# RWKV-7 chunks with both heads of a pair in one instruction, and inverse roots on GpSimd

## The chip, the cores and the metric

The kernel runs as one program on one core of a Trainium2 chip. The metric is the device time of one execution in microseconds (us); several runs were timed and the median is used. Beside the timed runs there is one execution taken with the hardware profiler. All times of single instructions come from it.

## The reference, cut to what matters

Two layers are computed on an input of 1024 positions by 1024 channels in float32. Layer 0 (RG-LRU and HGRN2) is not touched by the change. Layer 1 is RWKV-7 time mixing: 16 heads of 64 channels, each with a 64 x 64 state that is updated position by position:

```python
def step(state, inp):
    r_t, w_t, k_t, v_t, al_t, be_t = inp
    sa = jnp.einsum("bhvk,bhk->bhv", state, al_t)
    state = (state * w_t[:, :, None, :] + sa[..., None] * be_t[:, :, None, :]
             + v_t[..., None] * k_t[:, :, None, :])
    return state, jnp.einsum("bhvk,bhk->bhv", state, r_t)
...
y = ((y - mean) * lax.rsqrt(var + RW_GN_EPS)).reshape(bsz, seq, RW_WIDTH) * ln_w + ln_b
bonus = jnp.sum(r * k * r_k, axis=-1, keepdims=True) * v
y = y + bonus.reshape(bsz, seq, RW_WIDTH)
return (y * jax.nn.silu(g)) @ w_out
...
x = x + rms_norm(mix, post_norm[layer])
```

The mean and the variance of y are those of one head at one position.

## The kernel before, in words

The recurrence is not run position by position. The 1024 positions are cut into 16 chunks of 64, and within a chunk the recurrence is solved with matrix products and one inverted triangular 64 x 64 matrix per head. The heads are worked on in eight pairs; in a pair, head 0 lies on partitions 0 to 63 and head 1 on partitions 64 to 127. In the code `e` is the pair (0 to 7), `h` the head in the pair, `ch` the chunk.

Earlier stages (up to about 1380 us) have written to DRAM: `ard`, for each chunk the scaled vectors A (64 columns) and R (64 columns) of each head; `bkd`, the scaled vectors B and K, where head 0 has B in columns 0 to 63 and K in 64 to 127, and head 1 the other way round; `vd`, the values; and `abf`, from which `invert` and `merge` make the inverses `ytd` in the background. `egc` holds, for each chunk, the decay of each channel over the whole chunk.

The last stage is `chain_phase` (L1024). For each chunk it runs:

- `values` (L1399): loads the values into `SV` and the inverse into `YTc`. `SV` has for each head a stack of 128 partitions: the 64 rows of the state on the head's own half, the 64 values on the other half.
- `gram` (L1412), one chunk ahead: loads `GM` (A and R) and `BK`, and multiplies for each head BK against [A R] (L1428; 64 rows of contraction, 128 weight columns, 128 streamed columns, one PSUM bank per head and group of four pairs). VectorE masks the results with `gm`: the K part goes back into the other half of `GM` (L1433), the part that belongs to B and R into `RB` (L1434). These are four instructions for each group of four pairs, eight for a chunk. GpSimd scales BK by the chunk's decay into `BS` (L1438), and TensorE transposes `BS` (L1443); ScalarE copies it to `NK` (L1444).
- `chain` (L1447), the sequential part: since state and values are stacked, one product with 128 rows of contraction and 64 weight columns gives the right sides (L1456), and another of the same shape starts the outputs (L1461). ScalarE copies the right sides to `B` (L1458). GpSimd scales the old state into `se` (L1467, one instruction for each head). The inverse is applied (L1471), its result takes the values' place of the solved part in `SV` (L1473: head 0 by VectorE, head 1 by ScalarE). A product with `NK` (L1478) gives what the chunk adds to the state, and VectorE adds `se` and writes the next chunk's `SV` (L1480, one instruction for each head). The last product (L1483) completes the outputs, ScalarE copies them (L1486), and they go to DRAM.
- `norm` (L1492) normalizes the outputs of a chunk, `turn` (L1524) transposes them, and `project` (L1536) multiplies two chunks at a time by the output weights and adds the normalized result to x. Both use `rstd2` (L197) for 1/sqrt: a scaling on VectorE, a root on ScalarE (L202), a reciprocal and one Newton step on VectorE (L201, L203 to L206). There is also `rstd` (L189), used in layer 0: two GpSimd instructions (L193, L194), the second a power with exponent -0.5.

Each matrix product of float32 operands shows as two records in the profile, so the 16 products of a step (8 pairs, 2 heads) are 32 records; a transpose is one.

The order: `chain` and `gram` are generators, and `chain_phase` advances them in five steps per chunk. Between these it calls `background` (inverses and merges) and takes one piece of `fill`. The fill is the gate's projection (`gpiece`, L1014, products at L184 to L186) until chunk 8, and the output projection (`project`, L1550 to L1552) from chunk 9. The framework then orders each engine's instructions by a simulated timeline and these priorities, with raised priority for the chain of chunks 14 and 15. Each engine runs its list in order. PSUM has eight banks, shared out by `BANKS` (L1392); the load queue is SyncE's (SP).

Of the kernel before, what the change touches and what calls it, by code (L numbers as in the profile page):

```python
# [7 lines left out]
F32 = mybir.dt.float32  # L8
# [3 lines left out]
ALU = mybir.AluOpType  # L12
# [33 lines left out]
class Net:  # L46
# [977 lines left out]
    def chain_phase(self, cx, mp, vg, n):  # L1024


        nc, a = self.nc, self.a
# [20 lines left out]
        self.SV, self.YTc, self.G, self.Y, self.yd = {}, {}, {}, {}, [self.dram.tile([P, HALF], F32, name=f"yd{i}") for i in range(16)]  # L1048
# [8 lines left out]
        nc.gpsimd.memset(self.SV[0][0:64, 0], 0.0)  # L1057
        nc.gpsimd.memset(self.SV[0][64:128, 1], 0.0)
# [308 lines left out]
    def chain_consts(self):  # L1367
        nc, big = self.nc, self.big

        gm = big.tile([P, P], F32, name="gm")  # L1370
        for lo_, base in ((0, 0), (64, 64)):
            m = big.tile([P, P], F32, name="mask_g", tag="BS")
            mv = m.rearrange("p (a b) -> p a b", b=64)
            nc.gpsimd.memset(m, 1.0)
            nc.gpsimd.affine_select(out=mv, in_=mv, pattern=[[1, 2], [1, 64]], compare_op=ALU.is_ge, fill=0.0,
                                    base=base - 1, channel_multiplier=-1)
            nc.vector.tensor_copy(gm[lo_:lo_ + 64, :], m[lo_:lo_ + 64, :])
        self.gm = gm
# [13 lines left out]
    BANKS = {"pg": ("g", 2), "pt": ("t", 1), "pq": ("t", 1), "pi": ("t", 1), "pc": ("c", 2), "py": ("y", 1),  # L1392
# [18 lines left out]

    def gram(self, ch):  # L1412
        nc = self.nc
        GM = self.cc[ch % 2].tile([P, 2, KT, P], F32, name="GM")
        for h in range(2):
            hs = slice(64 * h, 64 * h + 64)
            nc.sync.dma_start(out=GM[hs, h], in_=self.ard[ch, hs])
        BK = self.big.tile([P, KT, P], F32, name="BK")
        nc.sync.dma_start(out=BK, in_=self.bkd[ch])
        RB = self.cc[ch % 2].tile([P, KT, 64], F32, name="RB")  # L1420
        bc = lambda x, n: x.rearrange("p (o t) -> p o t", o=1).broadcast_to([n, 4, x.shape[-1]])
        yield
        for eg in range(2):
            ps = [self.bank("pg").rearrange("p (q t) -> p q t", t=P) for _ in range(2)]
            for q in range(4):
                for h in range(2):
                    hs = slice(64 * h, 64 * h + 64)
                    nc.tensor.matmul(ps[h][:, q, :], lhsT=BK[hs, eg * 4 + q, :], rhs=GM[hs, h, eg * 4 + q, :],  # L1428
                                     start=True, stop=True)
            for h in range(2):  # L1430
                es = slice(eg * 4, eg * 4 + 4)
                b, k = slice(64 * h, 64 * h + 64), slice(64 - 64 * h, 128 - 64 * h)
                nc.vector.tensor_mul(GM[k, h, es, :], ps[h][k], bc(self.gm[k, :], 64))  # L1433
                nc.vector.tensor_mul(RB[b, es, :], ps[h][b, :, 64:128], bc(self.gm[b, 64:128], 64))  # L1434
            yield
        BS = self.big.tile([P, KT, P], F32, name="BS", tag="BS")
        eg_ = self.egc[:, ch, :].rearrange("p (e o) -> p e o", o=1).broadcast_to([P, KT, P])
        nc.gpsimd.tensor_mul(BS, BK, eg_)  # L1438
        NK = self.cc[ch % 2].tile([P, KT, P], F32, name="NK")
        for eg in range(2):  # L1440
            ps = self.bank("pt").rearrange("p (q t) -> p q t", t=P)
            for q in range(4):
                nc.tensor.transpose(ps[:, q, :], BS[:, eg * 4 + q, :], self.ident)  # L1443
            nc.scalar.copy(NK[:, eg * 4:eg * 4 + 4, :], ps)  # L1444
        self.G[ch] = GM, RB, NK

    def chain(self, ch):  # L1447
        nc = self.nc
        GM, RB, NK = self.G.pop(ch)
        SV, YT = self.SV.pop(ch), self.YTc.pop(ch)  # L1450
# [3 lines left out]
        ps = pv(self.bank("pc"))  # L1454
        for e, h in eh:
            nc.tensor.matmul(ps[H[h], e, :], lhsT=GM[:, h, e, 0:64], rhs=SV[:, h, e, :], start=True, stop=True)  # L1456
        B = self.cc[ch % 2].tile([P, KT, 64], F32, name="B")
        nc.scalar.copy(B, ps)  # L1458
        py = pv(self.bank("py"))
        for e, h in eh:  # L1460
            nc.tensor.matmul(py[H[h], e, :], lhsT=GM[:, h, e, 64:128], rhs=SV[:, h, e, :], start=(e == 0), stop=False,  # L1461
                             skip_group_check=True)
        if ch < 15:
            se = self.cc[ch % 2].tile([P, KT, 64], F32, name="se")
            for h in range(2):
                eg = self.egc[H[h], ch, :].rearrange("p (e o) -> p e o", o=1).broadcast_to([64, KT, 64])
                nc.gpsimd.tensor_mul(se[H[h]], SV[H[h], h], eg)  # L1467
        yield
        ps = pv(self.bank("pc"))
        for e, h in eh:  # L1470
            nc.tensor.matmul(ps[H[h], e, :], lhsT=YT[H[h], e, :], rhs=B[H[h], e, :], start=True, stop=True)  # L1471
        for h in range(2):
            (nc.scalar.copy if h else nc.vector.tensor_copy)(SV[H[h], h], ps[H[h]])  # L1473
        yield
        if ch < 15:
            ps = pv(self.bank("pc"))
            for e, h in eh:
                nc.tensor.matmul(ps[H[h], e, :], lhsT=NK[:, e, H[h]], rhs=SV[:, h, e, :], start=True, stop=True)  # L1478
            for h in range(2):
                nc.vector.tensor_add(self.SV[ch + 1][H[h], h], ps[H[h]], se[H[h]])  # L1480
        yield
        for e, h in eh:
            nc.tensor.matmul(py[H[h], e, :], lhsT=RB[H[h], e, :], rhs=SV[H[h], h, e, :], start=False, stop=(e == KT - 1),  # L1483
                             skip_group_check=True)
        y = self.cc[ch % 2].tile([P, HALF], F32, name="B")
        nc.scalar.copy(y, py.rearrange("p e v -> p (e v)"))  # L1486
# [5 lines left out]
    def norm(self, ch):  # L1492

        nc, gp = self.nc, self.gp
# [24 lines left out]
        r = self.rstd2(gp, va, KT, 1.0 / 64, GN_EPS)  # L1519
# [16 lines left out]
    def project(self, tt):  # L1536
# [28 lines left out]
        r = self.rstd2(gp, s1, 1, 1.0 / D, EPS)  # L1565
# [57 lines left out]
```

## Time and profile before

| | |
|---|---|
| median of 3 runs | 1886.89 us (1884.31 to 1889.57) |
| profiled execution, own time | 1885.01 us |
| its span, first to last instruction | 1882.9 us |
| TensorE matmul (PE) busy | 1737.0 us, 92% |
| TensorE weight load (PEld) busy | 1462.9 us, 78% |
| VectorE (DVE) busy | 1212.2 us, 64% |
| ScalarE (ACT) busy | 795.6 us, 42% |
| GpSimd (POOL) busy | 695.8 us, 37% |

How to read it: a row of the groups view names a line of the kernel, the engine, the operation, `out<-in`, the shapes and the count, and then the busy time in us, the mean of one instruction in ns, and the engine's idle time before them with what ended it. A TensorE shape such as `64*128 64x128` means 64 rows of contraction by 128 weight columns, and 64 rows by 128 streamed columns. Matmul records overlap, since the unit is pipelined: the time that a group takes is read from its start to the start of what follows, not from the records' lengths. PEclk is the share of its full clock that TensorE was granted.

### The profile page before, as it was taken

How to read it: one execution, taken by the hardware profiler on the slowest of the kernel's cores; microseconds unless marked ns; L12 is line 12 of the kernel's file. 1: busy time of each engine (PE TensorE's matmuls, PEld its weight loads, DVE VectorE, ACT ScalarE, POOL GpSimd, SP SyncE). 2: the span in 40 equal slices, each digit the busy share in tenths (PEclk: the TensorE clock that was granted, in tenths of full speed). 3: DMA queues.
4: the chain of work that ended last, by engine and by line, in shares of the span. 5: the costliest groups of instructions: out<-in, count | busy, mean ns of one | idle time of the engine just before them, and what ended most of it. 6: DMA issues, size and time to landing. Idle time of an engine off the chain costs nothing. (4 is left out here: it accounts for less than half of the span.)

```text
span 1882.9 us, 36336 instructions
## 1 busy us (share of the span) xinstructions
PE 1737.0 (92%) x14418; PEld 1462.9 (78%) x14418; DVE 1212.2 (64%) x2213; ACT 795.6 (42%) x1550; POOL 695.8 (37%) x618
## 2 busy tenths in 40 slices
PE   8989989999899999999999999978679999997888
PEld 6879789787897777777878766668678998875776
DVE  6485483675847889745354686786593434359985
ACT  5322222323226655445454765764453433432221
POOL 5534232333222212465434244554441425425430
PEclk9999999999899999999999999979878998988989
DMA  5101101111022111365235276654565655544531
GB/s 181 45 23 46 56 19 63 46 35 41 18 73 85 53 60 67 125 238 169 101 123 185 89 171 167 173 130 113 121 164 139 170 148 165 156 132 150 181 106 62
DMA packets 218313, 206.56 MB, mean 110 GB/s; under 512 B 133280, under 2 KB 162208, under 8 KB 218144
## 3 DMA queue, kind: packets, MB, share of 16 engines
q1 hardware_dynamic: 216992, 200.04, 35.5%
q0 software_dynamic: 1152, 4.19, 0.7%
q8 instruction: 114, 1.87, 0.4%
q14 instruction: 55, 0.45, 0.1%
HBM read 136.22 MB, written 67.96 MB: 108 GB/s over the span
## 5 line engine op out<-in xcount | busy, mean ns | idle before, releaser
L135 POOL TENSOR_TENSOR wl<-w,wh 128x1024 fp32r<-128x1024 f32 x110 | 276.5, 2520 | 291.6 <-ACT wh L133 283.2
L160 PE MATMUL mm<-xh,wh 128*128 128x512 f32 x768 | 306.3, 400 | 0.2
L162 PE MATMUL mm<-xh,wl 128*128 128x512 f32 x768 | 305.3, 398 | 0.0
L161 PE MATMUL mm<-xl,wh 128*128 128x512 f32 x768 | 304.1, 396 | 0.0
L184 PE MATMUL mm<-wh,xh 128*128 128x256 f32 x560 | 169.8, 304 | 7.5 <-ACT xh L149 3.7
L160 PEld LDWEIGHTS mm<-xh,wh 128*128 128x128 f32 x768 | 146.0, 190 | 35.3 <-issue 3.6
L162 PEld LDWEIGHTS mm<-xh,wl 128*128 128x128 f32 x768 | 145.9, 190 | 34.5 <-issue 4.1
L161 PEld LDWEIGHTS mm<-xl,wh 128*128 128x128 f32 x768 | 145.9, 190 | 33.2 <-issue 3.4
L186 PE MATMUL mm<-wh,xl 128*128 128x256 f32 x560 | 166.4, 300 | 4.9 <-DVE xl L150 4.9
L133 ACT CAST wh<-w 128x1024 fp32r<-128x1024 f32 x112 | 117.7, 1051 | 124.2 <-PE mm L161 54.8
L185 PE MATMUL mm<-wl,xh 128*128 128x256 f32 x560 | 165.7, 296 | 0.0
L184 PEld LDWEIGHTS mm<-wh,xh 128*128 128x128 f32 x560 | 114.5, 205 | 10.7 <-ACT xh L149 4.3
L186 PEld LDWEIGHTS mm<-wh,xl 128*128 128x128 f32 x560 | 113.6, 204 | 7.0 <-DVE xl L150 6.3
L185 PEld LDWEIGHTS mm<-wl,xh 128*128 128x128 f32 x560 | 114.2, 204 | 0.9
L803 DVE SCALAR_TENSOR_TENSOR mix<-ut,vec,mix 128x512 f32<-128x512 f32 x64 | 62.5, 985 | 39.9 <-ACT mix L802 39.1
L1438 POOL TENSOR_TENSOR BS<-BK,egc 128x1024 f32<-128x1024 f32 x16 | 31.7, 1980 | 139.5 <-PE pt L1443 70.7
L184 PE MATMUL po<-wh,xh 128*128 128x256 f32 x256 | 75.7, 296 | 1.6 <-DVE vg L1021 1.6
L420 DVE COPY_PREDICATED ST<-m_l,sm 64x128 f32<-64x128 uint8 x224 | 72.5, 337 | 5.5
L185 PE MATMUL po<-wl,xh 128*128 128x256 f32 x256 | 75.2, 294 | 0.0
L186 PE MATMUL po<-wh,xl 128*128 128x256 f32 x256 | 74.8, 292 | 0.0
L1428 PE MATMUL pg<-GM,BK 64*128 64x128 f32 x512 | 58.0, 308 | 9.4 <-DMA BK<-bkd 4.8
L1295 DVE TENSOR_TENSOR PR<-YP,BL 128x64 f32<-128x64 f32 (+14 forms) x60 | 57.5, 973 | 11.2 <-POOL BL L1285 10.4
(378 smaller groups left out, 4332.6 us busy)
## 6 DMA issues: line engine op xcount, KB each, us to landing
w<-in_W SPq DMA_DIRECT2D x112, 512.0 KB, 3.8
ard<-AR SPq DMA_DIRECT2D x16, 512.0 KB, 4.1
BK<-bkd SPq DMA_DIRECT2D x16, 512.0 KB, 3.7
vd<-vg SPq DMA_DIRECT2D x32, 256.0 KB, 2.7
GM<-ard SPq DMA_DIRECT2D x32, 256.0 KB, 4.4
x<-in_x SPq DMA_DIRECT2D x8, 512.0 KB, 9.8
mgd<-sgq SPq DMA_DIRECT2D x16, 256.0 KB, 2.1
ut<-mgd SPq DMA_DIRECT2D x16, 256.0 KB, 4.1
```

What stands on the lines that cost most here:

```text
L133: nc.scalar.copy(hi, w)
L135: (nc.vector if first else nc.gpsimd).tensor_sub(lo, w, hi.bitcast(F32))
L160: nc.tensor.matmul(ps, lhsT=wh[:, c:c + P], rhs=a, start=(k == 0), stop=False)
L161: nc.tensor.matmul(ps, lhsT=wh[:, c:c + P], rhs=b, start=False, stop=False)
L162: nc.tensor.matmul(ps, lhsT=wl[:, c:c + P], rhs=a, start=False, stop=(k == KT - 1))
L184: nc.tensor.matmul(ps, lhsT=a, rhs=h, start=(k == 0), stop=False)
L185: nc.tensor.matmul(ps, lhsT=a, rhs=l, start=False, stop=False)
L186: nc.tensor.matmul(ps, lhsT=b, rhs=h, start=False, stop=(k == KT - 1))
L420: nc.vector.copy_predicated(d, m, x)
L803: nc.vector.scalar_tensor_tensor(out, sh, self.v(f"mu{p}", k), out, ALU.mult, ALU.add)
L1295: nc.vector.tensor_mul(fv(PR, 0, [[16 * n, 2], [n, 16], [1, n]]), fv(YP, 0, [[256, 2], [16, 16], [1, n]]), fv(BL, i, [[256, 2], [0, 16], [ ...
L1428: nc.tensor.matmul(ps[h][:, q, :], lhsT=BK[hs, eg * 4 + q, :], rhs=GM[hs, h, eg * 4 + q, :], start=True, stop=True)
```

## The change

The masks now cover both heads, so that a PSUM bank that holds both is masked by one instruction. `gram` multiplies in two steps: K against [A R] (64 weight columns, 128 streamed), both heads into one bank, masked by one instruction per group of four pairs into `KG`; and B against R (64 by 64) for all eight pairs into one bank, masked by one instruction into `RB`. For head 1 the halves of [A R] are swapped when loaded, with two loads. The scaling of BK is gone: BK itself is transposed, and not for the last chunk. State and values are no longer stacked: `V` has the values, `UV` the values and the solved part, and one tile `S` the state of both heads. In `chain`, each head has a PSUM bank `pa[h]`. A product with `KG` (64 rows of contraction, 128 weight columns, 64 streamed) starts right sides and outputs at once, and one with `AR` and `S` adds the state's share (not in chunk 0). Copies of right sides and outputs are one instruction per head on ScalarE, as both copies of the solved part are now. The state is updated by one add and one multiplication for both heads on VectorE. `norm` and `project` call `rstd` in the place of `rstd2`. The banks: "pc" has one buffer in the place of two, "py" two in the place of one.

```diff
 chain_phase:
-        nc.gpsimd.memset(self.SV[0][0:64, 0], 0.0)
-        nc.gpsimd.memset(self.SV[0][64:128, 1], 0.0)
 chain_consts:
-        for lo_, base in ((0, 0), (64, 64)):
-            m = big.tile([P, P], F32, name="mask_g", tag="BS")
+        rm = big.tile([P, 64], F32, name="rm")
+        for lo_, base, step in ((0, -1, 1), (64, 64, -1)):
+            m = big.tile([P, P], F32, name="mask_g")
...
+            nc.vector.tensor_copy(rm[lo_:lo_ + 64, :], m[lo_:lo_ + 64, 64 - lo_:128 - lo_])
+        self.gm, self.rm = gm, rm
+        self.S = big.tile([P, KT, 64], F32, name="S")
-    BANKS = {"pg": ("g", 2), "pt": ("t", 1), "pq": ("t", 1), "pi": ("t", 1), "pc": ("c", 2), "py": ("y", 1),
+    BANKS = {"pg": ("g", 2), "pt": ("t", 1), "pq": ("t", 1), "pi": ("t", 1), "pc": ("c", 1), "py": ("y", 2),
 values:
-            o = 64 - 64 * h
-            nc.sync.dma_start(out=SV[o:o + 64, h].rearrange("p e v -> p (e v)"),
-                              in_=self.vd[ch * 64:(ch + 1) * 64, 0, h * HALF:(h + 1) * HALF])
+            src = self.vd[ch * 64:(ch + 1) * 64, 0, h * HALF:(h + 1) * HALF]
+            for v, o in ((V, 64 * h), (UV[:, h], 64 - 64 * h)):
+                nc.sync.dma_start(out=v[o:o + 64].rearrange("p e v -> p (e v)"), in_=src)
 gram:
-            nc.sync.dma_start(out=GM[hs, h], in_=self.ard[ch, hs])
+        nc.sync.dma_start(out=AR[H[0]], in_=self.ard[ch, H[0]])
+        for x in range(2):
+            nc.sync.dma_start(out=AR[H[1], :, H[1 - x]], in_=self.ard[ch, H[1], :, H[x]])
...
-                    nc.tensor.matmul(ps[h][:, q, :], lhsT=BK[hs, eg * 4 + q, :], rhs=GM[hs, h, eg * 4 + q, :],
+                    nc.tensor.matmul(ps[H[h], q, :], lhsT=BK[H[h], e, H[1 - h]], rhs=AR[H[h], e, :],
                                      start=True, stop=True)
+            nc.vector.tensor_mul(KG[:, es, :], ps, bc(self.gm, 4))
+        yield
+        ps = self.bank("pg").rearrange("p (e t) -> p e t", t=64)
+        for e in range(KT):
             for h in range(2):
-                nc.vector.tensor_mul(GM[k, h, es, :], ps[h][k], bc(self.gm[k, :], 64))
-                nc.vector.tensor_mul(RB[b, es, :], ps[h][b, :, 64:128], bc(self.gm[b, 64:128], 64))
-            yield
-        nc.gpsimd.tensor_mul(BS, BK, eg_)
+                nc.tensor.matmul(ps[H[h], e, :], lhsT=BK[H[h], e, H[h]], rhs=AR[H[h], e, H[1 - h]],
+                                 start=True, stop=True)
+        nc.vector.tensor_mul(RB, ps, bc(self.rm, KT))
+        yield
+        if ch < 15:
-                nc.tensor.transpose(ps[:, q, :], BS[:, eg * 4 + q, :], self.ident)
+                    nc.tensor.transpose(ps[:, q, :], BK[:, eg * 4 + q, :], self.ident)
 chain:
+        pa = [pv(self.bank("py")) for _ in range(2)]
         for e, h in eh:
-            nc.tensor.matmul(ps[H[h], e, :], lhsT=GM[:, h, e, 0:64], rhs=SV[:, h, e, :], start=True, stop=True)
+            nc.tensor.matmul(pa[h][:, e, :], lhsT=KG[H[h], e, :], rhs=V[H[h], e, :], start=(e == 0), stop=False,
+                             skip_group_check=True)
+        if ch:
+            for e, h in eh:
+                nc.tensor.matmul(pa[h][:, e, :], lhsT=AR[H[h], e, :], rhs=S[H[h], e, :], start=False, stop=False,
+                                 skip_group_check=True)
-        nc.scalar.copy(B, ps)
-        py = pv(self.bank("py"))
-        for e, h in eh:
-            nc.tensor.matmul(py[H[h], e, :], lhsT=GM[:, h, e, 64:128], rhs=SV[:, h, e, :], start=(e == 0), stop=False,
-                             skip_group_check=True)
-                nc.gpsimd.tensor_mul(se[H[h]], SV[H[h], h], eg)
+        for h in range(2):
+            nc.scalar.copy(B[H[h]], pa[h][H[h]])
...
-            (nc.scalar.copy if h else nc.vector.tensor_copy)(SV[H[h], h], ps[H[h]])
+            nc.scalar.copy(UV[H[h], h], ps[H[h]])
...
-                nc.tensor.matmul(ps[H[h], e, :], lhsT=NK[:, e, H[h]], rhs=SV[:, h, e, :], start=True, stop=True)
-            for h in range(2):
-                nc.vector.tensor_add(self.SV[ch + 1][H[h], h], ps[H[h]], se[H[h]])
+                nc.tensor.matmul(ps[H[h], e, :], lhsT=NK[:, e, H[h]], rhs=UV[:, h, e, :], start=True, stop=True)
+            if ch:
+                nc.vector.tensor_add(S, ps, S)
+            eg = self.egc[:, ch, :].rearrange("p (e o) -> p e o", o=1).broadcast_to([P, KT, 64])
+            nc.vector.tensor_mul(S, S if ch else ps, eg)
...
-            nc.tensor.matmul(py[H[h], e, :], lhsT=RB[H[h], e, :], rhs=SV[H[h], h, e, :], start=False, stop=(e == KT - 1),
+            nc.tensor.matmul(pa[h][H[1 - h], e, :], lhsT=RB[H[h], e, :], rhs=UV[H[h], h, e, :], start=False, stop=(e == KT - 1),
                              skip_group_check=True)
-        nc.scalar.copy(y, py.rearrange("p e v -> p (e v)"))
+        for h in range(2):
+            nc.scalar.copy(y[H[h]], pa[h][H[1 - h]])
 norm, project:
-        r = self.rstd2(gp, va, KT, 1.0 / 64, GN_EPS)
+        r = self.rstd(gp, va, KT, 1.0 / 64, GN_EPS)
-        r = self.rstd2(gp, s1, 1, 1.0 / D, EPS)
+        r = self.rstd(gp, s1, 1, 1.0 / D, EPS)
```

`rstd`, which they now call, was there before:

```python
r = pool.tile([P, n], F32, name="rstd")
nc.gpsimd.tensor_scalar(r, ss, scale, eps, ALU.mult, ALU.add)
nc.gpsimd.tensor_tensor(r, r, self.mhalf[:, 0:n], ALU.pow)
```

More of the change, by code (lines that the diff above doesn't have):

```diff
@@ L1047, in chain_phase @@
         self.solves = [self.solve_pairs(i) for i in (0, 2)]
-        self.SV, self.YTc, self.G, self.Y, self.yd = {}, {}, {}, {}, [self.dram.tile([P, HALF], F32, name=f"yd{i}") for i in range(16)]
+        self.V, self.YTc, self.G, self.Y, self.yd = {}, {}, {}, {}, [self.dram.tile([P, HALF], F32, name=f"yd{i}") for i in range(16)]
         g0, g1 = (self.mix_parts(mp, 3, th, nc.gpsimd) for th in range(2))
@@ L1370, in chain_consts @@
         gm = big.tile([P, P], F32, name="gm")
-        for lo_, base in ((0, 0), (64, 64)):
-            m = big.tile([P, P], F32, name="mask_g", tag="BS")
+        rm = big.tile([P, 64], F32, name="rm")
+        for lo_, base, step in ((0, -1, 1), (64, 64, -1)):
+            m = big.tile([P, P], F32, name="mask_g")
             mv = m.rearrange("p (a b) -> p a b", b=64)
             nc.gpsimd.memset(m, 1.0)
-            nc.gpsimd.affine_select(out=mv, in_=mv, pattern=[[1, 2], [1, 64]], compare_op=ALU.is_ge, fill=0.0,
-                                    base=base - 1, channel_multiplier=-1)
+            nc.gpsimd.affine_select(out=mv, in_=mv, pattern=[[step, 2], [1, 64]], compare_op=ALU.is_ge, fill=0.0,
+                                    base=base, channel_multiplier=-1)
             nc.vector.tensor_copy(gm[lo_:lo_ + 64, :], m[lo_:lo_ + 64, :])
-        self.gm = gm
+            nc.vector.tensor_copy(rm[lo_:lo_ + 64, :], m[lo_:lo_ + 64, 64 - lo_:128 - lo_])
+        self.gm, self.rm = gm, rm
+        self.S = big.tile([P, KT, 64], F32, name="S")
     def output_consts(self):
@@ L1418, in gram @@
         BK = self.big.tile([P, KT, P], F32, name="BK")
         nc.sync.dma_start(out=BK, in_=self.bkd[ch])
+        KG = self.cc[ch % 2].tile([P, KT, P], F32, name="KG")
         RB = self.cc[ch % 2].tile([P, KT, 64], F32, name="RB")
-        bc = lambda x, n: x.rearrange("p (o t) -> p o t", o=1).broadcast_to([n, 4, x.shape[-1]])
+        bc = lambda x, n: x.rearrange("p (o t) -> p o t", o=1).broadcast_to([P, n, x.shape[-1]])
         yield
         for eg in range(2):
-            ps = [self.bank("pg").rearrange("p (q t) -> p q t", t=P) for _ in range(2)]
+            es = slice(eg * 4, eg * 4 + 4)
+            ps = self.bank("pg").rearrange("p (q t) -> p q t", t=P)
@@ L1437, in gram @@
[L1437 to L1445, printed above, removed]
+                nc.tensor.matmul(ps[H[h], e, :], lhsT=BK[H[h], e, H[h]], rhs=AR[H[h], e, H[1 - h]],
+                                 start=True, stop=True)
@@ new lines, in gram @@
+        nc.vector.tensor_mul(RB, ps, bc(self.rm, KT))
+        yield
+        NK = None
+        if ch < 15:
+            NK = self.cc[ch % 2].tile([P, KT, P], F32, name="NK")
+            for eg in range(2):
+                ps = self.bank("pt").rearrange("p (q t) -> p q t", t=P)
+                for q in range(4):
+                    nc.tensor.transpose(ps[:, q, :], BK[:, eg * 4 + q, :], self.ident)
+                nc.scalar.copy(NK[:, eg * 4:eg * 4 + 4, :], ps)
+        self.G[ch] = AR, KG, RB, NK
@@ L1447, in chain @@
     def chain(self, ch):
         nc = self.nc
-        GM, RB, NK = self.G.pop(ch)
-        SV, YT = self.SV.pop(ch), self.YTc.pop(ch)
+        AR, KG, RB, NK = self.G.pop(ch)
+        (V, UV), YT, S = self.V.pop(ch), self.YTc.pop(ch), self.S
         H = [slice(0, 64), slice(64, 128)]
```

22 lines of the change are left out of this document (8 added, 14 removed).

## Prediction

> **What bounds the kernel now.** I read the busy rows of the page first, then a table of busy time by stretch for the stage that is changed (the chunks start at about 1380 us and run to the end), then the waits and the timeline inside it.
>
> ```profile
> span 1882.9 us, 36336 instructions
> core 0: us, PE busy (x) PEld busy (x) DVE busy (x) ACT busy (x) POOL busy (x), PEclk, DMA share, GB/s
> 1380.00:1454.00 74.00, 65.05 (x905) 60.59 (x901) 47.01 (x73) 31.48 (x68) 22.77 (x14) 0.90 0.61 163
> 1454.00:1630.00 176.00, 173.40 (x3098) 159.65 (x3096) 72.74 (x133) 70.27 (x160) 67.02 (x53) 0.97 0.55 155
> 1630.00:1674.00 44.00, 37.51 (x715) 32.41 (x713) 16.41 (x29) 16.51 (x37) 17.14 (x15) 0.84 0.54 156
> 1674.00:1825.00 151.00, 129.02 (x1370) 103.23 (x1368) 133.24 (x235) 39.21 (x91) 64.90 (x46) 0.91 0.45 143
> 1825.00:1883.00 58.00, 49.20 (x288) 36.80 (x288) 32.21 (x71) 11.77 (x30) 4.35 (x3) 0.91 0.22 77
> ```
>
> The stretches have two different limits. From 1454 to 1630 (chunks 1 to 8, filled with the gate's projection) TensorE is busy 173.40 of 176 us at 0.97 of its clock, and VectorE only 72.74: whatever TensorE gets on top there is paid. From 1674 to 1825 (chunks 10 to 15, filled with the output projection) VectorE is busy 133.24 of 151 us, TensorE stands still for 151 - 129.02 = 22 us, and at clock 0.91 it loses up to 0.09 x 151 = 13.6 us more. There VectorE is the limit. The waits of that stretch say who holds TensorE up:
>
> ```profile
> ACT SV L1473 <- DVE SV L1473: 16.4, 3, 7.8
> PE pc L1478 <- DVE SV L1473: 9.2, 3, 4.4
> PE pt L1443 <- DVE yl L150: 6.1, 2, 5.9
> ```
>
> The timeline of one such wait:
>
> ```profile
> 1725.25 2.42 DVE L1568 SCALAR_TENSOR_TENSOR x<-o,rr,x 128x512 f32<-128x512 f32 x2
> 1727.20 1.62 POOL L1509 TENSOR_TENSOR V<-V,G 128x512 f32<-128x512 f32 x1
> 1727.59 1.25 DVE L205 SCALAR_TENSOR_TENSOR rt<-rt,rv 128x8 f32<-128x8 f32 x1
> 1728.77 1.89 POOL L1438 TENSOR_TENSOR BS<-BK,egc 128x1024 f32<-128x1024 f32 x1
> 1728.87 1.82 DVE L206 SCALAR_TENSOR_TENSOR rr<-rt,rr 128x8 f32<-128x8 f32 x1
> 1732.36 0.67 DVE L1473 COPY SV<-pc 64x512 f32<-64x512 f32 x1
> 1733.09 0.29 PEld L1478 LDWEIGHTS pc<-SV,NK 128*64 128x64 f32 x2 [4.84 <-DVE SV L1473]
> ```
>
> The copy that the chain needs (L1473) is queued behind the roots' small steps, and each of these lasts as long as the GpSimd instruction beside it: L206, eight columns, takes 1.82 us while GpSimd runs BS. The change takes BS away, those steps and the copy from VectorE.
>
> **The change, TensorE first.** The slots, as start to start in the saturated stretch:
>
> ```profile
> 1506.76 1.15 PE L1471 MATMUL pc<-B,YTc 64*64 64x64 f32 x32
> 1507.84 0.49 PE L1428 MATMUL pg<-GM,BK 64*128 64x128 f32 x4
> ...
> 1512.57 1.16 PE L1428 MATMUL pg<-GM,BK 64*128 64x128 f32 x16
> 1513.66 0.45 PE L1483 MATMUL py<-SV,RB 64*64 64x64 f32 x8
> ...
> 1526.30 1.15 PE L1456 MATMUL pc<-SV,GM 128*64 128x64 f32 x32
> 1527.28 0.63 PE L1461 MATMUL py<-SV,GM 128*64 128x64 f32 x14
> L1428 PEld LDWEIGHTS pg<-GM,BK x512: 182/188/335, 1381.8 to 1815.2; 64*128 64x128 f32 x171
> L1471 PEld LDWEIGHTS pc<-B,YTc x512: 129/135/223, 1403.8 to 1846.7; 64*64 64x64 f32 x171
> ```
>
> A step of 32 records costs 0.98 us at L1456 and 1.08 us at L1471 (64 weight columns, 64 streamed), and 2 x 1.09 = 2.18 us at L1428 (128 and 128).
>
> The first product of `gram` keeps its 128 streamed columns with 64 weight columns: I take 2.18 us as before, so nothing. The second, B against R, is new: 64*64 with 64 streamed, as L1471, 1.08 us a chunk, 16 x 1.08 = 17.3 us.
>
> The product of KG with the values and that of AR with the state take the place of L1456 and L1461, one for one. They stream 64 columns but load 128 weight columns, a shape that the trace does not show at length. A load of 128 columns lasts 182 - 129 = 53 ns longer than one of 64. At 64 by 64 the 16 pairs of records (both heads overlap) come every 0.98 / 16 = 61 ns. If loads and streams overlap but the longer one sets the pace, each pair grows by 53 ns: 16 x 0.053 = 0.85 us a step. There are 16 KG steps and 15 AR steps: 26.3 us. The bounds: nothing, if the load hides; 2.18 - 0.98 = 1.20 us a step, 37.2 us, if a step costs what L1428 costs. I take 26.3, from the loads' own rows. It also could not be below nothing, since no row with 128 weight columns is shorter than its 64-column fellow.
>
> Chunk 0 has no AR step (-0.98 us), chunk 15 no transposes, eight records that I put at about the same (-1.0). Sum for TensorE at full clock: 17.3 + 26.3 - 2 = 41.6 us more. A chunk inside gets 1.08 + 2 x 0.85 = 2.8 us, so the eight chunks from 1454 to 1630 get 22 us and the five from 1674 to 1825 get 14.
>
> A rule speaks against the change at one point. The first product used one PSUM bank per head; now both heads, which are different row tiles of the array, write one bank, as the new product does. The row is L1471, where both heads already write the one bank `pc`: 32 records in 1.08 us, 34 ns each, against 31 ns at L1456. The Trainium skill, TensorEngine Tiling (Array Packing), Restrictions and Gotchas, says that different row tiles cannot access the same PSUM bank simultaneously. By that rule the heads would take turns. The trace does not agree where the heads write different partitions, so the sum goes without it; it is a rival below.
>
> **VectorE, GpSimd, ScalarE.**
>
> ```profile
> L1433 DVE TENSOR_TENSOR GM<-pg,gm 64x512 f32<-64x512 f32 x20 | 13.7, 685 | 0.3
> L1434 DVE TENSOR_TENSOR RB<-pg,gm 64x256 f32<-64x256 f32 x20 | 8.4, 422 | 1.5 <-PE py L1483 1.2
> L1480 DVE TENSOR_TENSOR SV<-pc,se 64x512 f32<-64x512 f32 x9 | 6.2, 686 | 0.2
> L1473 DVE COPY SV<-pc 64x512 f32<-64x512 f32 x5 | 3.4, 674 | 0.0
> L206 DVE SCALAR_TENSOR_TENSOR rr<-rt,rr 128x8 f32<-128x8 f32 x11 | 5.8, 527 | 0.2
> L205 DVE SCALAR_TENSOR_TENSOR rt<-rt,rv 128x8 f32<-128x8 f32 x11 | 3.1, 281 | 0.1
> L1520 DVE TENSOR_TENSOR yn<-yn,rr 128x512 f32<-128x512 f32 x11 | 8.6, 781 | 0.2
> L1467 POOL TENSOR_TENSOR se<-SV,egc 64x512 f32<-64x512 f32 x30 | 31.8, 1059 | 28.2 <-DVE SV L1480 27.1
> L1438 POOL TENSOR_TENSOR BS<-BK,egc 128x1024 f32<-128x1024 f32 x16 | 31.7, 1980 | 139.5 <-PE pt L1443 70.7 <-issue 51.3 <-DMA A<-abf 17.2
> L194 POOL TENSOR_TENSOR rstd<-rstd,mhalf 128x4 f32<-128x4 f32 x16 | 16.2, 1013 | 1.0
> L194 POOL TENSOR_TENSOR rstd<-rstd,mhalf 128x1 f32<-128x1 f32 x24 | 14.2, 593 | 1.9
> L193 POOL TENSOR_SCALAR rstd<-ms 128x4 f32<-128x4 f32 x16 | 3.1, 193 | 32.3 <-DVE ms L552 22.4 <-DVE cpos L610 9.4
> L1458 ACT COPY B<-pc 128x512 f32<-128x512 f32 x16 | 9.4, 585 | 12.7 <-issue 7.6 <-PE pc L1456 4.9
> ```
>
> The VectorE rows are those of 1674 to 1825. An instruction over 64 partitions costs what one over 128 does at equal columns, so two heads in one is half. Of its 133.24 us go 13.7 + 8.4 + 6.2 + 3.4 = 31.7, and at least 5.8 + 3.1 = 8.9 of the roots. To it come, for five chunks, three masks of 0.685 (10.3 us), an add of 0.686 and a multiplication priced as L1520, 0.781 (7.3 us). That leaves about 110 of 151 us: no longer the limit.
>
> GpSimd loses 31.8 + 31.7 = 63.5 us. It gains 16 roots of eight columns: by the rows of one and four columns (1013 - 593) / 3 = 140 ns a column, 593 + 7 x 140 = 1573, with the scaling 1.77 us; and 8 roots of one column, 0.79 us; 34.6 us in all. A root queues with the next norm's three products on GpSimd, and VectorE's multiplication with it waits. Two chunks of norms run ahead of the projection, so I count nothing until the tail. There the last norm lies beside a half of the projection, and the last root stands bare: 0.79 us against six small steps, nothing, bounds 1 us either way.
>
> ScalarE gains a half copy each of B, of the solved part and of y, 3 x 0.585 = 1.8 us a chunk, beside 39.21 of 151 us: hidden. The chain is longer by three such copies, and the next KG step waits until both y copies have left `pa`; while the fill covers it, nothing, and 1.8 us a chunk where it is bare. SP gets three more loads a chunk, a chunk ahead of their use: nothing. BK's load now waits for the transposes in the place of BS:
>
> ```profile
> BK<-bkd SPq DMA_DIRECT2D x16, 512.0 KB, 3.7
> ```
>
> Both come at the end of the same step of `gram`, so I count nothing; bare it would be its 3.7 us a chunk.
>
> **The sum.** What of TensorE's waits comes back, stage by stage: 1380 to 1454, 1 us; 1454 to 1630, 4 of 2.6 idle and 5.3 clock, since TensorE does not wait for VectorE there; 1630 to 1674, 2; 1674 to 1825, where the two VectorE waits above are 9.2 + 6.1 = 15.3, I take 13 of these and 6 of the 13.6 of clock that follow them, 19; the end 1. That is 27 us. The profiled execution took 1885.01 us, 2.1 over its span and 1.9 under the median of 1886.89. 1885.01 + 41.6 - 27 = 1899.6, say 1899 us. About 0.3%, 5.7 us, is what a measurement of this kernel can tell from no change.
>
> **Rivals.**
> - VectorE's relief wins: faster. Between 1674 and 1825 all 22 + 13.6 us come back, and 10 to 19 in the other stretches (where 9.0 + 6.5 + 8.8 stand idle before and after the saturated one): 46 to 54 us, 1885 + 41.6 - 50 = 1877. For it: VectorE at 133 of 151 us and the copy at 1732.36; against it: the 14 us more of that stretch need the same gaps, and the 22 us more of chunks 1 to 8 find nothing idle. It decides from 42 us recovered. 0.20.
> - The 128 weight columns cost nothing: -26.3, 1873 us. For it: the loads of both heads overlap already. Against it: 53 ns a load more in the rows. 0.12.
> - The new waits eat the relief (roots on GpSimd hold VectorE as BS did at L206, 1.82 us; the bare copies; both `pa` banks busy): 10 recovered, 1917 us. 0.15.
> - The two heads take turns in a bank, by the rule above: an unpaired record of the first product at about twice the paired one doubles 1.08 a chunk, and the first product up to 2.18: some 2.4 us a chunk, 38 us, 1938. 0.03.
> - My forecast, 0.50.
>
> **How the numbers follow.** Low end: free columns with 5 us more recovered, 1868. High end: 37.2 in place of 26.3 with 15 recovered, 1885 + 52.5 - 15 = 1922. Outside lie the bank rule and the edges, under 2 in 10. Of the forecast 0.05 falls within 0.3%, of the relief 0.05 and of the free columns 0.03, and 0.03 of the eaten relief: faster 0.27, same 0.16, slower 0.57.
>
> **What would show it.** Right: KG and AR steps near 1.83 us of 32 records, the B against R product near 1.08 (34 ns a record); chunks 1 to 8 each some 2.5 us longer than their 176 / 8 = 22; from 1674 on VectorE under 115 us, hardly a wait of TensorE for VectorE, and a higher clock. Wrong: KG steps at 0.98 us; the late stretch shorter by over 20 us; or VectorE's instructions as long as the GpSimd root beside them.

## The result, and the profile after

The changed kernel takes 1959.71 us (median of 4 runs, 1952.47 to 1960.47) beside 1888.23 us for the kernel before in the same series (4 runs, 1884.31 to 1892.55). The ratio is 1.0369, with a 95% interval of 1.0335 to 1.0404. That is 70 us slower, where 12 were forecast and 1922 was the upper end of the range. The profiled execution took 1960.31 us, its span 1958.6.

First the table of busy time by stretch, of the changed kernel, cut at the same places of the work as the prediction's table: up to the first product of chunk 1, chunks 1 to 7, chunks 8 and 9, chunks 10 to 14, chunk 15 to the end. The columns are the stretch, its length, the busy time of PE, PEld, DVE, ACT and POOL with the number of instructions, the granted clock, the DMA share and GB/s.

```profile
span 1958.6 us, 37077 instructions
1380.00:1459.30 79.30, 61.33 (x884) 56.78 (x882) 37.07 (x54) 29.40 (x65) 21.76 (x14) 0.85 0.57 151
1459.30:1684.40 225.10, 192.23 (x3366) 177.91 (x3362) 50.55 (x84) 79.30 (x178) 37.31 (x30) 0.90 0.47 131
1684.40:1754.70 70.30, 62.55 (x893) 53.69 (x892) 21.57 (x33) 25.36 (x55) 20.41 (x18) 0.88 0.45 127
1754.70:1904.40 149.70, 137.91 (x1406) 112.25 (x1405) 80.76 (x118) 39.90 (x77) 66.33 (x63) 0.87 0.49 152
1904.40:1959.00 54.60, 40.33 (x270) 32.92 (x269) 18.72 (x31) 11.11 (x24) 6.64 (x10) 0.91 0.14 54
```

The time was not lost where VectorE had been the bound. Chunks 10 to 14 take 149.7 us, before 151: VectorE falls from 133.24 to 80.76 us and TensorE's idle time from 22 to 149.70 - 137.91 = 11.8, but the clock falls too, from 0.91 to 0.87. Chunks 1 to 7, saturated before (176 us, clock 0.97), now take 225.1 us at clock 0.90, and TensorE stands idle for 225.10 - 192.23 = 32.9 us in them, where it was 2.6. Chunks 8 and 9 go from 44 to 70.3 us, partly with work that lay later before: TensorE has 893 records in them in place of 715, and only 64 of the 178 more are the new product's. So these stages are read together: chunks 8 to 14 took 44 + 151 = 195 us and now take 70.30 + 149.70 = 220.0, though TensorE's idle time in them falls from 28.5 to 19.5 us.

What TensorE waits for from 1380 us on, the costliest rows of the waits of the changed kernel (total us, times, longest):

```profile
PE pg L1436 <- DMA BK<-bkd: 28.1, 9, 6.4
PE pi L1357 <- ACT A L1351: 9.0, 1, 9.0
PE pi L1348 <- DVE X L1341: 8.0, 2, 5.8
PE po L184 <- DVE vg L1021: 7.4, 1, 7.4
PE pe L1544 <- DVE B L1533: 5.9, 1, 5.9
```

The waits for VectorE that the prediction wanted gone (L1478 for the copy of the solved part, 9.2 us) are gone. In their place stands the load of BK. The timeline of one chunk of the changed kernel, the rows that touch BK and the loads ahead of it in SyncE's queue (start, length, what ran; in brackets the idle time before it and what ended it):

```profile
1531.37 0.60 PE L1453 MATMUL pt<-ident,BK 128*128 128x128 f32 x4
1532.00 0.59 ACT L1454 COPY NK<-pt 128x512 f32<-128x512 f32 x1 [0.16 <-PE pt L1453]
1532.42 1.11 SPq L1409 DMA_DIRECT2D V<-vd  x2
1533.62 0.55 SPq L1421 DMA_DIRECT2D AR<-ard  x1
1534.22 1.26 SPq L1423 DMA_DIRECT2D AR<-ard  x2
1535.58 0.56 SPq L1425 DMA_DIRECT2D BK<-bkd  x1
1541.51 0.90 PE L1436 MATMUL pg<-AR,BK 64*64 64x128 f32 x5 [6.36 <-DMA BK<-bkd]
```

And of the kernel before, with the transposes of BS:

```profile
1517.25 0.60 PE L1443 MATMUL pt<-ident,BS 128*128 128x128 f32 x4
1518.00 1.89 POOL L1438 TENSOR_TENSOR BS<-BK,egc 128x1024 f32<-128x1024 f32 x1 [11.93 <-issue]
1520.24 0.39 SPq L1419 DMA_DIRECT2D BK<-bkd  x1
1525.25 0.49 PE L1428 MATMUL pg<-GM,BK 64*128 64x128 f32 x4
1537.00 0.66 PE L1443 MATMUL pt<-ident,BS 128*128 128x128 f32 x4
```

BK has one buffer in both kernels. Before, GpSimd's scaling was its last reader: it ended at 1519.89, the load went out 0.35 us later, and by the median of its kind (3.7 us to land) it was there when TensorE came to the product at 1525.25. The transposes of the scaled copy followed only at 1537.00. After, the transposes are the last reader. They come late in the chunk, and the first product of the next `gram` is planned soon behind: it starts when the load lands, and TensorE stands for 6.36 us. The hold is not all of it in this chunk. The transposes end at 1531.97, but the load goes out at 1535.58, behind two loads of V and three of AR in SyncE's queue; and a load of BK now takes 5.3 us to land by the median. What the added loads do to it was not measured by itself. What such a stop does to the clock is in the busy time of the two stretches around it, of the changed kernel (length, PE, PEld, DVE, ACT, POOL, clock, DMA share, GB/s):

```profile
1535.60:1541.50 5.90, 0.00 (x0) 0.00 (x0) 0.42 (x1) 1.38 (x3) 0.00 (x0) 0.80 0.80 211
1541.50:1546.00 4.50, 4.49 (x45) 3.94 (x47) 1.38 (x2) 0.00 (x0) 0.00 (x0) 0.50 0.00 0
```

For the 4.5 us after the stop TensorE works at half its clock, so the stop costs about 2 us more than it lasts. The Trainium skill, TensorE: Matmul & The Clock Gate, HAM oscillation, describes just this, a wait for a DMA after which the next tile starts at half rate; here the trace agrees with it, 0.50.

### The profile page after: what moved, and what is told of

Read it like the earlier page. It is cut to its first block, busy times and chain, and to the rows that moved or that the text cites. A ratio compares the mean times of both kernels' runs of the same rounds, so it can differ in the third digit from the quotient of the medians.

```text
span 1958.6 us, 37077 instructions
## 1 busy us (share of the span) xinstructions
PE 1778.4 (91%) x14890; PEld 1503.2 (77%) x14890; DVE 1119.2 (57%) x1998; ACT 812.4 (41%) x1567; POOL 665.7 (34%) x618
## 5 line engine op out<-in xcount | busy, mean ns | idle before, releaser
L184 PE MATMUL po<-wh,xh 128*128 128x256 f32 x256 | 80.2, 313 | 7.4 <-DVE vg L1021 7.4
L1436 PE MATMUL pg<-AR,BK 64*64 64x128 f32 x512 | 51.1, 341 | 28.8 <-DMA BK<-bkd 28.1
L1021 DVE TENSOR_TENSOR vg<-po,vg 128x256 f32<-128x256 f32 x32 | 13.5, 422 | 104.1 <-ACT vg L1020 100.6
L1436 PEld LDWEIGHTS pg<-AR,BK 64*64 64x64 f32 x512 | 41.2, 174 | 34.0 <-DMA BK<-bkd 25.8
```

The costliest lines, as they stand in the source:

```text
L184: nc.tensor.matmul(ps, lhsT=a, rhs=h, start=(k == 0), stop=False)
L1436: nc.tensor.matmul(ps[H[h], q, :], lhsT=BK[H[h], e, H[1 - h]], rhs=AR[H[h], e, :], start=True, stop=True)
```

## The experiments

The theory after the result: the load of BK, held until the transposes, is bare (not covered by other work) in nearly every chunk. Three rivals: TensorE's added work is paid in full and dearer than forecast; the roots on GpSimd delay norm, turn and tail; ScalarE's doubled copies and the chain's single bank `pc` make the chain slower.

Each result is given as its ratio to the kernel before in the same series; 0.01 is 19 us.

### Two buffers for BK in the changed kernel

So that memory is enough, NK is written over BK, half by half, after its transposes.

```diff
-        BK = self.big.tile([P, KT, P], F32, name="BK")
+        BK = self.cc[ch % 2].tile([P, KT, P], F32, name="BK")
...
-            NK = self.cc[ch % 2].tile([P, KT, P], F32, name="NK")
+            NK = BK
```

> The changed kernel with BK in two buffers (NK's copies are written over it, so that it takes no more memory); no engine's arithmetic changes. Theory (BK's single buffer, held to its transposes, makes the load bare in nearly every chunk): 35 to 50 us below the changed kernel, 1910 to 1925 us, and the row L1436 <- DMA BK loses most of its 28.1 us. Rival 1 (TensorE's added products, about 40 us, are the cost): within 8 us of the changed kernel, about 1955. Rival 2 (roots on GpSimd delay the chain): also within 8 us.

Measured: 1938.56 us (1933.78 to 1941.56), ratio 1.0258 (1.0228 to 1.0288). The wait has nearly gone; of this kernel's waits from 1380 us on:

```profile
PE pi L1348 <- DVE X L1341: 12.0, 3, 6.3
PE pg L1436 <- DMA BK<-bkd: 8.2, 5, 4.1
```

It gives 1.0369 - 1.0258 = 0.011, 21 us (give or take 9). The theory is right in kind and too large in size: it had 35 to 50. TensorE had waited for 9 of the loads, not for nearly all. Some 48 us are still open.

### BK held in the kernel before

```diff
-        BS = self.big.tile([P, KT, P], F32, name="BS", tag="BS")
+        BS = BK
```

> The kernel before with GpSimd's scaling written over BK instead of into BS: same instructions, but BK is now held until its transposes. Theory (the held load): 25 to 45 us above the kernel before, 1913 to 1933 us, with L1428 waiting for BK's load in most chunks. Rival 1 (added products) and rival 2 (roots): neither is in this kernel, so within 5 us of the kernel before.

Measured: 1915.72 us (1910.04 to 1920.30), ratio 1.0131 (1.0096 to 1.0165), 25 us slower with the same instructions. Its costliest wait is the one of the changed kernel:

```profile
PE pg L1428 <- DMA BK<-bkd: 32.8, 9, 5.7
```

So the price of the held load is shown from both sides: 21 us taken away, 25 put on. None of the other rivals has a part in this kernel. One thing more comes with this edit: a scaling that writes over BK must also follow the product that reads BK, so the 25 us hold what this order costs.

### The roots, alone and undone

In the kernel before `rstd` for `rstd2` in `norm` and `project`; in the changed kernel the reverse.

```diff
-        r = self.rstd2(gp, va, KT, 1.0 / 64, GN_EPS)
+        r = self.rstd(gp, va, KT, 1.0 / 64, GN_EPS)
```

> The kernel before with the roots alone moved to GpSimd (rstd for rstd2 in norm and project). Theory (the held load): no part in it; the tail's wait alone, 0 to 7 us above the kernel before. Rival 1 (products): within 7 us as well. Rival 2 (roots delay the chain): 20 us or more above.

> The changed kernel with the roots back in their old form on VectorE. Theory (the held load): 0 to 7 us below the changed kernel, by the turn of the last chunk that waits less; BK's wait stays near 28 us. Rival 1 (products): the same. Rival 2 (roots): 20 us or more below.

Measured: the roots alone 1886.05 us, ratio 0.9987 (0.9969 to 1.0006); the change without them 1959.24 us, ratio 1.0359 (1.0331 to 1.0387), beside 1.0369 with them. The roots cost and gain nothing that shows either way. The rival falls.

### 64 weight columns in the two steps that carry the change

The changed kernel with two BK buffers; KG and AR enter with the 64 columns that give the right sides. What the other 64 give to the outputs is left out, and the product with RB then starts the outputs' half of the bank (`start=(e == 0)`).

```diff
-nc.tensor.matmul(pa[h][:, e, :], lhsT=KG[H[h], e, :], rhs=V[H[h], e, :], ...
+nc.tensor.matmul(pa[h][H[h], e, :], lhsT=KG[H[h], e, H[h]], rhs=V[H[h], e, :], ...
...
-    nc.tensor.matmul(pa[h][:, e, :], lhsT=AR[H[h], e, :], rhs=S[H[h], e, :], ...
+    nc.tensor.matmul(pa[h][H[h], e, :], lhsT=AR[H[h], e, H[h]], rhs=S[H[h], e, :], ...
```

> The changed kernel with BK in two buffers (1938.6 us), and in it the KG and AR steps with 64 weight columns in place of 128; what the two steps would give to the outputs is left out. Same number of instructions. Rival 1 (what is left over the kernel before is TensorE's work): 31 steps x 0.85 us = 26 us less, 1912 us. Rival 3 (what is left is waits, on ScalarE's copies and the chain): within 8 us of 1938.6.

Measured: 1900.28 us (1892.96 to 1909.95), ratio 1.0053 (1.0028 to 1.0078), so 0.0205 or 38 us (give or take 7) below the same kernel with 128 columns. Steps in the timeline that run in one piece, first the changed kernel:

```profile
1904.37 2.00 PE L1467 MATMUL py<-V,KG 64*128 64x64 f32 x32
1906.20 1.95 PE L1471 MATMUL py<-S,AR 64*128 64x64 f32 x30
```

then the one with 64 columns:

```profile
1552.53 1.15 PE L1471 MATMUL py<-S,AR 64*64 64x64 f32 x32
1553.61 0.39 PE L184 MATMUL po<-wh,xh 128*128 128x256 f32 x1
```

Start to start a step takes 1906.20 - 1904.37 = 1.83 us with 128 columns and 1553.61 - 1552.53 = 1.08 with 64. That is 0.75 us, 23 us over 31 steps. The other 15 us lie in the same steps. TensorE's busy time at L1467 (KG) and L1471 (AR) alone, from 1380 us on (PE, PEld, clock, DMA share, GB/s), first with 128 columns:

```profile
1380.00:1932.10 552.10, 42.21 (x512) 37.28 (x512) 0.90 0.48 140
1380.00:1932.10 552.10, 45.32 (x480) 40.59 (x480) 0.90 0.48 140
```

then with 64:

```profile
1380.00:1903.40 523.40, 24.42 (x512) 20.97 (x512) 0.92 0.53 148
1380.00:1903.40 523.40, 23.71 (x480) 19.97 (x480) 0.92 0.53 148
```

Together 87.53 against 48.13, 39.4 us less. Thirty-one steps of 1.83 us would be 57 us, but most steps do not run in one piece: other products are planned in between (the last section shows what such a border costs), and behind a stop the clock is halved. How much each of these does was not measured. All engines from 1380 us on, first 128 columns, then 64:

```profile
1380.00:1932.10 552.10, 491.15 (x6806) 427.49 (x6804) 205.77 (x317) 185.22 (x400) 152.55 (x134) 0.90 0.48 140
```

```profile
1380.00:1903.40 523.40, 443.72 (x6863) 388.76 (x6862) 212.98 (x323) 189.21 (x408) 153.16 (x134) 0.92 0.53 148
```

Some of the gain comes back as idle time of TensorE, 79.7 us in place of 61.0. The two profiled executions lie 1933.78 - 1905.10 = 28.7 us apart, less than the medians, so the 38 rest on the medians.

### The same in the kernel with one BK buffer

> The changed kernel (1959.7 us), BK in one buffer, with 64 weight columns in the KG and AR steps; what they would give to the outputs is left out. If the load's price and the weights' add up: 38 us less, 1922. If the faster steps are eaten by waits for BK: less than 25 us less, above 1935.

Measured: 1926.46 us (1909.70 to 1931.10), ratio 1.0180 (1.0145 to 1.0214), which is 0.0189 or 36 us (give or take 9) below the changed kernel. The two prices add up.

### The new product alone

In the kernel before, one more step of 32 records per chunk, in the shape of the new product of B and R, which nothing reads.

```diff
+        H = [slice(0, 64), slice(64, 128)]
+        ps = self.bank("pg").rearrange("p (e t) -> p e t", t=64)
+        for e in range(KT):
+            for h in range(2):
+                nc.tensor.matmul(ps[H[h], e, :], lhsT=BK[H[h], e, H[h]], rhs=BK[H[h], e, H[1 - h]],
+                                 start=True, stop=True)
         BS = self.big.tile([P, KT, P], F32, name="BS", tag="BS")
```

> The kernel before with one more step of 32 products (64 by 64, 64 streamed) in each chunk, which nothing reads: the cost of the new product of B and R by itself. Rival 1 (TensorE's work is paid in full): 16 x 1.08 = 17 us above the kernel before, up to 25 with the changes of shape around the step; Rival 3 (TensorE's gaps take it): 0 to 8 us.

Measured: 1901.39 us (1898.27 to 1902.03), ratio 1.0065 (1.0040 to 1.0089): 12 us (give or take 5), between the two expectations. It agrees with what is left of the changed kernel when load and weights are undone, 0.0053 or 10 us.

### VectorE's relief, taken away and given

Two experiments ask what VectorE's time is worth. The first puts the relief back out of the changed kernel with two BK buffers (1.0258): masks, adds and scalings once for each head.

```diff
-            nc.vector.tensor_mul(KG[:, es, :], ps, bc(self.gm, 4))
+            for g in H:
+                nc.vector.tensor_mul(KG[g, es, :], ps[g], bc(self.gm, 4)[g])
```

(and so for `RB` and for both instructions on `S`).

> The changed kernel with BK in two buffers (1938.6 us), and in it each of VectorE's masks, adds and scalings split into one for each head again: it undoes one part of the change, 77 instructions more and some 50 us of VectorE. If the relief was worth the prediction's 27 us, or a good part of it: 15 us or more above 1938.6. If it was worth nothing: within 6 us.

The second gives relief to the kernel before: one head's masks are left out, and loads fill what they would write.

```diff
-            for h in range(2):
+            for h in range(1):
                 es = slice(eg * 4, eg * 4 + 4)
...
+        nc.sync.dma_start(out=GM[0:64, 1], in_=self.ard[ch, 0:64])
+        nc.sync.dma_start(out=RB[64:128], in_=self.ard[ch, 64:128, :, 0:64])
```

> The kernel before with the masks of one head left out (32 of 64 instructions L1433 and L1434, some 35 us of VectorE over the chunks); the places that they write are filled by two loads a chunk instead, so the numbers are not masked for that head. TensorE's work is unchanged. If VectorE's relief comes back on the path, as the prediction's 27 us had it: 12 to 20 us below the kernel before. If TensorE and the order of the chain set the pace: within 5 us.

Measured: the split 1938.82 us, ratio 1.0265 (1.0233 to 1.0296), beside 1.0258; half the masks 1892.31 us, ratio 1.0027 (1.0008 to 1.0047). The rows from 1380 us on, split first, then half the masks (VectorE is the third busy time):

```profile
1380.00:1940.50 560.50, 497.16 (x6828) 432.49 (x6827) 264.50 (x398) 187.30 (x403) 155.09 (x134) 0.89 0.48 138
```

```profile
1380.00:1890.90 510.90, 454.60 (x6344) 391.82 (x6343) 264.73 (x474) 169.89 (x384) 176.41 (x129) 0.91 0.54 154
```

The split puts 264.50 - 205.77 = 59 us on VectorE, and the time stays (0.0007, give or take 0.0042, or 8 us). In the other kernel VectorE is relieved of 37 us (301.60 before), and it becomes no faster; it has two loads more, which may cover a few us of gain. In these two kernels time on VectorE does not set the end.

### ScalarE's copies and the chain's bank

Three runs on the last rival. One of each pair of copies back to VectorE, in the changed kernel with two BK buffers:

```diff
-            nc.scalar.copy(UV[H[h], h], ps[H[h]])
+            (nc.scalar.copy if h else nc.vector.tensor_copy)(UV[H[h], h], ps[H[h]])
```

(and so for `B` and `y`).

> The changed kernel with BK in two buffers (1938.6 us), and in it one of each pair of copies (B, UV, y) moved from ScalarE to VectorE, 47 copies. Rival 3 (the waits on ScalarE's doubled copies are what is left): 10 to 20 us less, 1920 to 1928. Rival 1 (TensorE's work): within 6 us of 1938.6.

The reverse in the kernel before, both copies of the solved part on ScalarE, with the roots on GpSimd:

> The kernel before with only two parts that cost TensorE nothing: both copies of the solved part on ScalarE, and the roots on GpSimd. If VectorE's queue holds the chain (the waits L1478 <- DVE SV L1473 of 9.2 us, and 16.4 us of ScalarE behind the same copy): 10 to 20 us below the kernel before, 1870 to 1880. If that relief is worth nothing on the path: within 5 us.

And the kernel before with `"pc": ("c", 1)` in place of 2:

> The kernel before with one bank pc in place of two; nothing else. If one bank makes the chain's steps wait for each other's copies: 8 to 20 us above the kernel before, with waits of L1456, L1471 and L1478 for the copies that empty the bank. If not: within 4 us.

Measured: 1942.05 us, ratio 1.0295 (1.0254 to 1.0336), no gain; 1901.73 us, ratio 1.0070 (1.0030 to 1.0110), 13 us slower where 10 to 20 faster were expected; 1885.52 us, ratio 0.9979 (0.9961 to 0.9998). One bank `pc` costs nothing in the kernel before. Both copies of the solved part on ScalarE, with the roots on GpSimd, made the kernel before slower; since the roots alone cost nothing, it is the copies or a new order of the engines' lists. Giving VectorE one copy of each pair in the changed kernel did not help. There the chain then waits for VectorE's copy:

```profile
PE pc L1479 <- DVE B L1475: 16.8, 5, 5.2
```

### The tail, and a version that is faster than both

In the changed kernel the last chunk's root stands in GpSimd's queue behind the projection's. The timeline of its tail:

```profile
1932.53 0.19 POOL L193 TENSOR_SCALAR rstd<-s 128x1 f32<-128x1 f32 x1 [9.53 <-DVE s L1576]
1932.80 0.20 POOL L193 TENSOR_SCALAR rstd<-va 128x8 f32<-128x8 f32 x1
1933.07 2.17 POOL L194 TENSOR_TENSOR rstd<-rstd,mhalf 128x1 f32<-128x1 f32 x2
1935.28 0.69 DVE L1532 TENSOR_TENSOR B<-B,rstd 128x512 f32<-128x512 f32 x1 [0.20 <-POOL rstd L194]
1936.84 1.09 PE L1544 MATMUL pe<-ident,B 128*128 128x128 f32 x4 [5.91 <-DVE B L1533]
```

The scaling of the last norm waits its turn at L193 until the projection's sum is there, and TensorE waits 5.91 us. So the last root, and in the changed kernel the projection's roots too, went back to VectorE.

> The changed kernel with BK in two buffers (1938.6 us), with the last norm's root and the projection's roots back on VectorE. If the tail's wait, PE pe L1544 <- DVE B L1533 of 5.9 us, is bare: 5 to 9 us less, 1930 to 1934. If the tail is bound elsewhere: within 3 us.

> The kernel before, BK in one buffer, norm's roots on GpSimd for all chunks but the last. If the 12 us that the kernel with two buffers gained came from the roots and the tail alone: 8 to 13 us below the kernel before, about 1878. If the second buffer is needed for it: within 4 us of the kernel before.

> The kernel before with BK in two buffers and NK written over it. The waits L1428 <- DMA BK and <- issue, 7.1 us, go, with some of the clock after them: 4 to 10 us below the kernel before, 1881 to 1887 us. If these waits lie under others: within 3 us.

> The same, and the roots of norm on GpSimd for all chunks but the last, whose root stays on VectorE, so that the turn at the end does not wait its 6 us. 4 to 8 us below the kernel with BK in two buffers alone, 1875 to 1881; if the roots on GpSimd bring nothing before the tail, the same as that one.

> The kernel before with BK in two buffers and norm's roots on GpSimd in all chunks, the last too (the kernel with the last root on VectorE: 1877.2 us). If the tail's wait of 6 us is bare: 1881 to 1885. If the gain is one of order and not of the roots: 1886 to 1892, near the kernel before.

| kernel | us | ratio |
|---|---|---|
| changed, two BK buffers, last root on VectorE | 1937.39 | 1.0260 (1.0242 to 1.0278) |
| before, roots but the last on GpSimd | 1892.35 | 1.0018 (1.0007 to 1.0029) |
| before, two BK buffers | 1888.99 | 1.0006 (0.9988 to 1.0024) |
| before, two BK buffers, roots but the last | 1877.20 | 0.9941 (0.9919 to 0.9962) |
| before, two BK buffers, all of norm's roots | 1881.60 | 0.9949 (0.9929 to 0.9968) |

The tail's wait does not show in the time, though it is bare in the trace: 1.0260 beside 1.0258 in the changed kernel, 0.9949 beside 0.9941 in the kernel before. Each of these differences is known to about 6 us only, so a gain of a few us is not ruled out. Two buffers alone gain nothing in the kernel before, the roots alone nothing, both together 10 to 11 us; the fourth row beats both kernels. The waits of the kernel before with two buffers hold a hint:

```profile
PE pc L1456 <- DVE SV L1480: 9.7, 5, 4.8
PE po L1550 <- ACT yh L149: 8.5, 2, 7.7
```

With the roots on GpSimd as well, all but the last, the second of these waits is 0.8 us. Each edit also lets the framework order the engines' lists anew. Whether the pair gains by two waits that lie over each other, or by a lucky order, stays open.

## Why the prediction was wrong

The direction was right; the size lay outside the range. By the steps:

- **"Both come at the end of the same step of `gram`, so I count nothing; bare it would be its 3.7 us a chunk."** This step failed first. That the two readers come at the end of the same generator step says nothing about time. GpSimd scaled BK as soon as the transposes of the chunk before had left BS (they end at 1517.85, the scaling starts at 1518.00), and the transposes of that scaled copy came only at 1537.00. So the change moved the release of BK back by much of a chunk. Before, the load landed, by its median, at 1520.24 + 3.7 = 1523.9, 1.3 us ahead of its use; that thin cover was the row to look up. The held load costs 21 to 25 us, not the 15 x 3.7 = 56 of its bare price, since some chunks still cover it.
- **"That is 27 us" recovered from TensorE's waits for VectorE.** This failed too: on the whole kernel nothing measurable came back, by the split (0, give or take 8 us) and by the half masks (0.0027 slower). The rows were right, and the waits for VectorE did go. In chunks 10 to 14 VectorE stands at 80.76 us where under 115 was forecast, and TensorE's idle time falls by 10 us. But the clock there fell to 0.87, where a higher one was forecast, and TensorE waits for others. The costliest rows of the changed kernel from 1754.7 to 1904.4 us:

```profile
PE pg L1436 <- DMA BK<-bkd: 6.8, 2, 6.4
PE pt L1453 <- ACT NK L1454: 4.1, 2, 3.0
```

  A wait's releaser is only the last to come, so the wait that it names can go while others take its place.
- **The 128 weight columns, "I take 26.3".** A step in one piece was forecast at 1.83 us and takes 1.83 us. Yet the two steps cost 38 us (give or take 7) as measured on the whole kernel, and 36 (give or take 9) with one BK buffer, about the upper bound of 37.2. The term was mis-sized: it priced steps that run in one piece, and in the kernel most are broken up.
- **The product of B and R, 17.3 us.** Its step takes what was forecast; on the whole kernel it costs 12 us (give or take 5). Whether TensorE's gaps take a part of it stays open.
- The roots, the half copies on ScalarE, the loads of AR and of the values: "nothing" held for the roots (0.9987). For the copies, undoing them in the changed kernel gave nothing, but putting those of the solved part, with the roots, into the kernel before cost 13 us. The added loads had no run of their own.
- Of the signs that were named, one speaks plainly: chunks 1 to 7 should each have grown by some 2.5 us, and grew by (225.10 - 176) / 7 = 7.0.
- The rule on PSUM banks, a rival at 0.03, is out. In the changed kernel the new product, both heads in one bank:

```profile
1578.70 1.10 PE L1443 MATMUL pg<-AR,BK 64*64 64x64 f32 x32
1579.73 0.39 PE L184 MATMUL po<-wh,xh 128*128 128x256 f32 x1
```

  1.03 us for 32 records, 32 ns each. The AR step of the kernel with 64 weight columns has the same shape and a bank for each head, and takes 1.08 us: sharing the bank costs nothing. What the Trainium skill, TensorEngine Tiling (Array Packing), Restrictions and Gotchas, says of row tiles and one bank doesn't show when they write different partitions.
- A slip without weight: 1454 to 1630 us are seven chunks (1 to 7), not eight, and 1674 to 1825 are chunks 10 to 14.

The sum with the measured terms: 21 (load) + 38 (weights) + 10 (product, and all the rest) = 69 us, the measured 70. The first two are differences between runs, and the third is what the kernel without them still has over the one before, so the three give the whole by construction. What checks them are the separate runs: 25 us for the held load, 36 for the weights, 12 for the product alone. Of the 58 us between the forecast of 12 and the measured 70, the relief that did not come is 27, the load 21 and the weights 12; the product, 5 under its forecast, and the noise of each term make up the rest. The rival "the new waits eat the relief" had the right form, but the waits it named were the roots, the copies and the banks; the load, which was written down with its price, had been set to nothing.

## What to carry to other kernels

When an edit changes which instruction reads a single-buffered tile last, follow the load: when is it released, when does it land, when is it used, and how many tenths of a microsecond lie between. And a wait row names the last of several that were late; ask what is late next before its time is written down as a gain, or test it by putting the work back (59 us on VectorE here, and the time stayed). The weight columns of a TensorE step were a price here even at equal instruction counts, and a step priced in one piece was too cheap for a kernel that runs it in several.

## What the runs showed of the hardware

A switch between a product that uses 64 rows and one that uses 128 is not free. In the changed kernel with two BK buffers the framework puts four transposes (128 rows) between a KG and an AR step (64 rows), and four more into the AR step; the first 6 records of the KG step ran earlier:

```profile
1568.10 1.77 PE L1467 MATMUL py<-V,KG 64*128 64x64 f32 x26
1569.80 0.66 PE L1453 MATMUL pt<-ident,BK 128*128 128x128 f32 x4
1570.39 1.77 PE L1471 MATMUL py<-S,AR 64*128 64x64 f32 x26
1572.09 0.66 PE L1453 MATMUL pt<-ident,BK 128*128 128x128 f32 x4
1572.68 0.66 PE L1471 MATMUL py<-S,AR 64*128 64x64 f32 x6
1573.26 0.38 PE L184 MATMUL po<-wh,xh 128*128 128x256 f32 x1
```

26 records at 1.83 / 32 = 57 ns would take 1.49 us; from the start of the group to that of the transposes it is 1569.80 - 1568.10 = 1.70, 0.2 us more for the change of shape. The AR step with its 32 records lies between 1570.39 and 1573.26, when the next product starts. That is 2.87 us, 0.59 of them the transposes; 2.28 are left, where the unbroken step takes 1.83. The Trainium skill, TensorEngine Tiling (Array Packing), Key Properties, says that a change of the tiling mode drains TensorE; the trace agrees, at about 0.2 us a change. The kernel before has borders too: in the prediction's timeline, 14 records of L1461 (128 rows, 64 weight columns) start at 1527.28, and in the same trace the next product, with 32 rows, starts at 1527.84; that is 0.56 us, where the 31 ns a record of L1456 would give 0.43. Whether the change brings more or dearer borders, and what they cost in sum, was not measured by itself.

GpSimd's root of eight columns, which the kernel before did not have, was estimated at 1573 ns for its second instruction; in the tail above the two roots, one and eight columns, take 2.17 us together, so 0.59 for the one column leaves 1.58. The mean of all 16 in the changed kernel is 1671 ns.
